# Moving one convolution tap and one query projection in the second layer of a four-layer hybrid model

## The chip, the cores and the metric

The kernel runs on one core of a Trainium2 chip. The metric is the device time of one execution in microseconds (us). The kernel before was timed three times: median 2625.26 us, lowest 2623.77, highest 2625.77. A profile of one more execution, which took 2624.74 us, records each instruction by engine: TensorE (PE, its weight loads PEld), VectorE (DVE), ScalarE (ACT), GpSimdE (POOL) and SyncE's DMA queue (SP). Lines such as L856 are lines of the kernel before.

## The reference

Four layers run over 1040 positions (16 learned ones ahead of 1024 inputs) of width 1024. Each normalises its input, mixes along the sequence, and adds its output. Layers 1 and 4 are sliding window attention, layer 3 is a gated linear recurrence, and layer 2, the one concerned here, is an mLSTM with eight heads. Cut to what matters of it:

```python
def causal_conv(x, w, b):                       # four taps along the sequence
    K = w.shape[0]
    L = x.shape[1]
    xp = jnp.pad(x, ((0, 0), (K - 1, 0), (0, 0)))
    return sum(xp[:, j:j + L] * w[j] for j in range(K)) + b

q, k, v, ig, fg, og, z = _split(u @ w_in, B_SIZES)
qk = jax.nn.silu(causal_conv(jnp.concatenate([q, k], axis=-1), conv_w, conv_b))
...
h = mlstm_chunkwise(qh, kh, vh, log_i, log_f)   # blocks of 128, a state C carried from block to block
h = jax.nn.sigmoid(og) * h
h = rmsnorm(h, h_gain)
return (h * jax.nn.silu(z)) @ w_out
```

## The kernel before, in words

All values are kept transposed, features on the 128 partitions and positions along the free axis. The positions are cut into three chunks of 400, 384 and 256 columns, which hold the blocks 0 to 3, 4 to 6 and 7 to 8 (block 0 has 16 positions, the others 128). A projection (`proj`, L211) makes one tile of 128 features: for each chunk 24 matmuls of 128x128 weights (L228, three products of split operands for each eighth of the input) into one PSUM bank, and then its evacuation function. PSUM has eight banks, handed out by one pool to everything that needs one. Weights are loaded by SP in two halves, then split by ScalarE (the rounded part, `wh`) and VectorE (the remainder, `wl`) at L194 and L195; each of the two has three buffers.

**Order of the work.** TensorE's order is written out by hand: a list of steps, each with a cost, a function and perhaps a weight load to be issued 12 us of cost ahead. `weave` merges two lists in proportion to their costs, `later` puts single steps in at given costs. The instructions of the other engines are put in order when the program is built, by priority (the order in which the code issues them) and by when the build expects their inputs; the steps of a mixer are issued with a priority 40 places ahead. On the chip each engine then works through its order as it stands, and waits where an input is missing.

**A query or key tile** of head h (`conv_proj`, L836) is one projection. The evacuation of a chunk takes a temporary `raw` of three columns more than the chunk. VectorE puts into these three the end of the chunk before (L849, zeros for the first, L847). ScalarE copies the chunk from PSUM into `raw` (L850). VectorE makes the last tap and the bias from it (L853), then adds the three other taps (L856, three times). Then SiLU: ScalarE L400 to L402 (abs, exp, ln), VectorE L403, ScalarE L404 (exp), and the product on VectorE (L860 for queries, L862 with a constant for keys). `raw` and the temporary of the SiLU come from a ring of six. Query tiles have two buffers, key tiles come from a ring of eight rows.

**The mixer of a head** (`mixer`, L875) works on nine blocks. `start` loads two rows, broadcast over the partitions (L881, L882). For each block: s1, the scores k*q (L889) and a transpose of k (L891), and beside it the decay E (VectorE L893, ScalarE L895), W = E times scores (VectorE L897), the scaled queries qw (L900) and keys kw (ScalarE L903). s2, the output product from W (L910) and from the state C (L912), and its normalisation (L914 to L918). s3, the state update: a product (L924) and C on VectorE (L927 for the first block, L929). s4, two transposes (L938) and copies (L940). On TensorE the steps of neighbouring blocks overlap: s1(0), s1(1), s2(0), s3(0), s1(2), s2(1), s3(1), s4(0), and so on.

**The start of the layer.** The head of the layer projects the values of head 0 and the gates (L277). Then come the query and the key tile of head 0, with three steps put in by `later`: the last gate transposes (`gate_turn`), the gate rows (`gate_rows`, L801 to L819: one long row per head on 8 partitions, on ScalarE and VectorE, then written to memory for the broadcasts), and 17 us of cost later the gate columns (`gate_cols`, L829 to L834). Then the mixer of head 0, all but its last three steps, is woven with the query, key and value projections of head 1, and so on for each head.

Of the kernel before, what the change touches and what calls it, by code (L numbers as in the profile page):

```python
# [11 lines left out]
AF = mybir.ActivationFunctionType  # L12
ALU = mybir.AluOpType
# [42 lines left out]
def weave(a, b):  # L56

    ta, tb = sum(x[0] for x in a) + 1e-9, sum(x[0] for x in b) + 1e-9
    out, i, j, ca, cb = [], 0, 0, 0.0, 0.0
    while i < len(a) or j < len(b):  # L60
        if j >= len(b) or (i < len(a) and ca / ta <= cb / tb):
            ca += a[i][0]
            out.append(a[i])
            i += 1
        else:
            cb += b[j][0]
            out.append(b[j])
            j += 1
    return out


def flat(groups):
    return [x for grp in groups for x in grp]
# [13 lines left out]
def later(steps, *events):  # L87

    k, t = 0, 0.0
    for delay, step in events:  # L90
        while k < len(steps) and (t < delay or steps[k][0] == 0.0):
            t += steps[k][0]
            k += 1
        steps.insert(k, step)
        t += step[0]
        k += 1
# [15 lines left out]
def hybrid_kernel(ctx: ExitStack, tc: tile.TileContext, ins, out, layers=(0, 1, 2, 3)):  # L112
    nc = tc.nc
    v, s, g, pe, sp = nc.vector, nc.scalar, nc.gpsimd, nc.tensor, nc.sync
# [11 lines left out]
    def nm(x):  # L126
        ctr[0] += 1
        return f"{x}{ctr[0]}"

    def row():  # L130
        return rpool.tile([P, T], F32, tag="r", name=nm("r"), bufs=ROWS)
# [7 lines left out]
    def tmp():  # L139
        return tpool.tile([P, 404], F32, tag="t", name=nm("t"), bufs=TMPS)  # L140
# [70 lines left out]
    def proj(src, evac, chunks=CHUNKS):  # L211
        st = {}

        def pre():
            st["w"] = weights(src, "m")

        groups = []
        for n, (c0, cn) in enumerate(chunks):
            grp = []
            for part in range(4):  # L220
                def fn(n=n, c0=c0, cn=cn, part=part):
                    if part == 0:
                        st[n] = psj()
                    h, l = st["w"]
                    acc = st[n]
                    for k in (2 * part, 2 * part + 1):
                        for i, (a, b) in enumerate(((h, uh), (h, ul), (l, uh))):
                            pe.matmul(acc[:, :cn], a[:, k, :], b[:, k, c0 : c0 + cn],  # L228
                                      start=(k == 0 and i == 0), stop=(k == KT - 1 and i == 2))
                    if part == 3:  # L230
                        evac(acc, n, c0, cn)

                grp.append([6 * cn * MM, fn, pre if (n == 0 and part == 0) else None])
            groups.append(grp)
        return groups
# [9 lines left out]
    def proj_v(srcs, evac, kind="v"):  # L245

        st = {}
        nc = 256 if kind == "v" else 272
        pieces, k = [], 0
        for src in srcs:  # L250
            n = src.shape[-1] // nc
            pieces.append((k, n, src))
            k += n

        groups = []
        for blocks in CHUNK_BLOCKS:
            grp = []
            for b in blocks:
                c0, cn = blk(b)
                for i, (k0, kn, src) in enumerate(pieces):  # L260
                    def pre(i=i, src=src):
                        st[i] = weights(src, kind)

                    def fn(b=b, c0=c0, cn=cn, i=i, k0=k0, kn=kn):
                        if i == 0:
                            st["a", b] = psj()
                        acc = st["a", b]
                        wh, wl = st[i]
                        for kk in range(kn):
                            k = k0 + kk  # L270
                            if b == 0:
                                for m in (wh, wl):
                                    pe.matmul(acc[:48, :nc], um[0][:, k, :], m[:, kk, :],
                                              start=(k == 0 and m is wh), stop=(k == KT - 1 and m is wl))
                            else:
                                for j, (a, m) in enumerate(((uh, wh), (uh, wl), (ul, wh))):
                                    pe.matmul(acc[:cn, :nc], a[:, k, c0 : c0 + cn], m[:, kk, :],  # L277
                                              start=(k == 0 and j == 0), stop=(k == KT - 1 and j == 2))
                        if i == len(pieces) - 1:
                            evac(acc, b, c0, cn)  # L280

                    grp.append([(2 if b == 0 else 3) * kn * nc * MM, fn, pre if b == 0 else None])
            groups.append(grp)
        return groups
# [113 lines left out]
    def sigmoid_from(z, cn):  # L398
        a = tmp()
        s.activation(a[:, :cn], z, AF.Abs)  # L400
        s.activation(a[:, :cn], a[:, :cn], AF.Exp, scale=-1.0)
        s.activation(a[:, :cn], a[:, :cn], AF.Ln, bias=one)  # L402
        v.scalar_tensor_tensor(a[:, :cn], z, 0.0, a[:, :cn], op0=ALU.min, op1=ALU.subtract)  # L403
        s.activation(a[:, :cn], a[:, :cn], AF.Exp)  # L404
        return a
# [351 lines left out]
    def layer_b(i, j, fin):  # L757
# [78 lines left out]
        def conv_proj(src, mt, mul, key):  # L836
            prev = [None, None]

            def evac(acc, n, c0, cn):
                conv = R["conv"]  # L840
                raw = tmp()
                if n == 0:
                    if mt < 8:
                        R[key] = R["mix"].tile([P, T], F32, tag="q", name=nm("q"), bufs=2)
                    else:
                        R[key] = row()
                    v.memset(raw[:, 0:3], 0.0)  # L847
                else:
                    v.tensor_copy(raw[:, 0:3], prev[0][:, prev[1] : prev[1] + 3])  # L849
                s.copy(raw[:, 3 : 3 + cn], acc[:, :cn])  # L850
                prev[:] = [raw, cn]
                y = R[key][:, c0 : c0 + cn]
                v.tensor_scalar(y, raw[:, 3 : 3 + cn], conv[:, mt, 3:4], conv[:, mt, 4:5],  # L853
                                op0=ALU.mult, op1=ALU.add)
                for q in (2, 1, 0):
                    v.scalar_tensor_tensor(y, raw[:, q : q + cn], conv[:, mt, q : q + 1], y,  # L856
                                           op0=ALU.mult, op1=ALU.add)
                a = sigmoid_from(y, cn)
                if mul == 1.0:
                    v.tensor_tensor(y, y, a[:, :cn], op=ALU.mult)  # L860
                else:
                    v.scalar_tensor_tensor(y, y, mul, a[:, :cn], op0=ALU.mult, op1=ALU.mult)  # L862

            return proj(src, evac)

        def v_evac(h):
            def f(acc, b, c0, cn):
                R["v", h, b] = V = vtile()
                put_v(V, acc, b, cn)
                if h == 0:  # L870
                    gate_evac(acc, b, cn)
                g.memset(V[:cn, 256:257], 1.0)
            return f
# [120 lines left out]
        qg = {h: conv_proj(win[8 * h], h, 1.0, ("q", h)) for h in range(8)}  # L994
        kg = {h: conv_proj(win[8 * h + 1], 8 + h, 128 ** -0.5, ("k", h)) for h in range(8)}
        gsrc = [ins["b_wv0"][j][:, 272 * a : 272 * b] for a, b in ((0, 3), (3, 6), (6, 8))]
        vg = {h: proj_v([win[8 * h + 2], win[8 * h + 3]], v_evac(h)) if h else proj_v(gsrc, v_evac(0), "g") for h in range(8)}
# [14 lines left out]
        for n in (0, 1):  # L1012
            later(head[n + 1], (GATE_LAG, gate_turn(n)))
        head[0].insert(0, [0.0, enter, None])
        body = flat(qg[0]) + flat(kg[0])
        later(body, (GATE_LAG, gate_turn(2)), (0.0, [0.0, gate_rows, None]), (GATE_COLS, [18 * 30, gate_cols, None]))
        for h in range(8):
            mx = mixer(h)
            mx, rest = mx[:-3], mx[-3:]
            if h < 7:  # L1020
                body += weave(mx, flat(qg[h + 1]) + flat(kg[h + 1]) + flat(vg[h + 1]))
                if h < 6:
                    body += weave(rest, gates(h)[:6]) + gates(h)[6:] + flat(zg[h][1]) + flat(outs(oc[h]))
                else:
                    held = rest
            else:
                body += weave(held + mx, gates(6) + flat(zg[6][1]))
# [304 lines left out]
    for pos, i in enumerate(layers):  # L1332
# [10 lines left out]
        if i % 3 == 0:  # L1343
            head, body, oa, ob = layer_a(i, i // 3, tail is None, i == 3, fin)
        elif i % 3 == 1:
            head, body, oa, ob = layer_b(i, i // 3, fin)
        else:
            head, body, oa, ob = layer_c(i, i // 3, fin)
# [155 lines left out]
```

## Time and profile before

| | |
|---|---|
| median of three runs | 2625.26 us |
| the profiled execution | 2624.74 us |
| its span, first to last instruction | 2623.0 us |
| TensorE busy | 2565.2 us, 98% |
| VectorE busy | 1970.6 us, 75% |
| ScalarE busy | 1665.7 us, 64% |
| granted TensorE clock, mean | 0.993 of full |

How to read the profile. A group has line, engine, operation, output and inputs by the program's names, shape and count; then busy time and the mean duration in ns; then the engine's idle time just before, and what ended it. In a timeline a row is start, duration, engine, line and operation, with the idle time before it and its releaser in brackets. A wait row names who waited for whom, the total in us, how often, and the longest. Matmuls are pipelined: a row's duration is longer than the distance to the next one, so steps of TensorE are measured from start to start. Durations of neighbouring VectorE rows overlap by a little under 0.1 us.

### The profile page before, as it was taken

The page shows a single profiled execution, that of the slowest core. Times are in us where ns is not written, and L with a number is a line of the kernel's source. Part 1 is how long each engine was busy: PE and PEld are TensorE (multiplying, and loading weights), DVE is VectorE, ACT ScalarE, POOL GpSimd, SP SyncE. Part 2 cuts the span into 40 slices and gives each one's busy share as a digit, 9 for nine tenths or more (in the row PEclk, how much of TensorE's full clock was granted, in tenths as well). Part 3 has the DMA queues.
Part 4 walks back from the last instruction along what each step waited for, and adds up shares of the span by engine and source line. Part 5 has one row for each costly group of instructions (what it writes and reads, how often), then busy time and mean ns, then how long its engine had stood idle before and what let it go on. Part 6 is the DMA issues. An engine that isn't in the chain of part 4 may idle for free. (4 is left out here: it accounts for less than half of the span.)

```text
span 2623.0 us, 54248 instructions
## 1 busy us (share of the span) xinstructions
PE 2565.2 (98%) x20422; PEld 2484.6 (95%) x20422; DVE 1970.6 (75%) x5296; ACT 1665.7 (64%) x4374; POOL 249.8 (10%) x502
## 2 busy tenths in 40 slices
PE   7999999989999999999999999999999999999999
PEld 5999999989999999999999999999999999999999
DVE  6798798784747474747475688989787978887996
ACT  6776767565454545454545657878585857767772
POOL 2221221000000000000000000100000100321330
PEclk9999999999999999999999999999999999999999
DMA  4212111021111111111111101011110112212112
GB/s 129 68 50 84 55 44 48 22 66 49 42 56 41 57 41 56 42 53 45 53 45 49 49 26 50 26 42 34 34 42 30 38 51 86 59 50 84 55 39 79
DMA packets 82583, 135.92 MB, mean 52 GB/s; under 512 B 12033, under 2 KB 35713, under 8 KB 82321
## 3 DMA queue, kind: packets, MB, share of 16 engines
q1 hardware_dynamic: 82320, 132.45, 16.2%
q8 instruction: 161, 2.64, 0.4%
q14 instruction: 102, 0.83, 0.1%
HBM read 117.56 MB, written 4.26 MB: 46 GB/s over the span
## 5 line engine op out<-in xcount | busy, mean ns | idle before, releaser
L228 PE MATMUL pj<-uh,wh 128*128 128x256 f32 (+2 forms) x2688 | 916.4, 341 | 9.6 <-ACT uh L194 9.6
L228 PE MATMUL pj<-ul,wh 128*128 128x256 f32 (+2 forms) x2688 | 867.9, 323 | 2.2 <-DVE ul L195 1.7
L228 PE MATMUL pj<-uh,wl 128*128 128x256 f32 (+2 forms) x2688 | 864.6, 322 | 0.0
L228 PEld LDWEIGHTS pj<-uh,wh 128*128 128x128 f32 x2688 | 510.2, 190 | 26.8 <-ACT uh L194 13.2
L228 PEld LDWEIGHTS pj<-ul,wh 128*128 128x128 f32 x2688 | 510.5, 190 | 11.1 <-DVE ul L195 5.8
L228 PEld LDWEIGHTS pj<-uh,wl 128*128 128x128 f32 x2688 | 510.0, 190 | 0.0
L194 ACT CAST wh<-wr 128x512 fp32r<-128x512 f32 (+1 forms) x338 | 203.2, 613 | 110.9 <-PE pj L322 32.7
L195 DVE TENSOR_TENSOR wl<-wr,wh 128x512 fp32r<-128x512 f32 (+1 forms) x338 | 233.7, 701 | 51.6 <-ACT wh L194 49.3
L325 DVE TENSOR_TENSOR x<-x,pj 128x384 f32<-128x384 f32 (+2 forms) x480 | 234.7, 508 | 35.0 <-PE pj L322 33.7
L322 PE MATMUL pj<-yh,wh 128*128 128x384 f32 (+2 forms) x768 | 253.0, 329 | 8.0 <-DVE x L325 6.2
L322 PE MATMUL pj<-yh,wl 128*128 128x384 f32 (+2 forms) x768 | 245.2, 319 | 0.0
L322 PE MATMUL pj<-yl,wh 128*128 128x384 f32 (+2 forms) x768 | 245.2, 319 | 0.0
L277 PE MATMUL pj<-wh,uh 128*128 128x256 f32 (+1 forms) x768 | 231.9, 302 | 0.0
L277 PE MATMUL pj<-wl,uh 128*128 128x256 f32 (+1 forms) x768 | 216.5, 282 | 0.0
L277 PE MATMUL pj<-wh,ul 128*128 128x256 f32 (+1 forms) x768 | 216.2, 281 | 0.0
L635 POOL TENSOR_TENSOR Sm<-Sm,s 128x512 f32<-128x512 f32 (+2 forms) x136 | 142.1, 1045 | 449.4 <-DVE s L634 434.5
L632 ACT ACTIVATE Sm<-Sm,s 128x257 f32<-128x257 f32 (+2 forms) x272 | 130.9, 482 | 79.5 <-DVE s L629 75.3
L404 ACT ACTIVATE t<-t 128x384 f32<-128x384 f32 (+2 forms) x240 | 117.9, 491 | 87.8 <-DVE t L403 86.0
L403 DVE SCALAR_TENSOR_TENSOR t<-pj,t 128x384 f32<-128x384 f32 (+2 forms) x192 | 98.7, 514 | 80.0 <-ACT t L402 78.1
L322 PEld LDWEIGHTS pj<-yh,wh 128*128 128x128 f32 x768 | 144.2, 188 | 11.7 <-DVE x L325 7.4
L194 ACT CAST yh<-r 128x384 fp32r<-128x384 f32 (+2 forms) x120 | 57.1, 478 | 151.9 <-PE pj L322 139.8
L277 PEld LDWEIGHTS pj<-wh,uh 128*128 128x128 f32 x768 | 144.6, 188 | 2.1
(255 smaller groups left out, 5423.0 us busy)
## 6 DMA issues: line engine op xcount, KB each, us to landing
wr<-in_b_win SPq DMA_DIRECT2D x124, 256.0 KB, 2.8
wr<-in_a_win SPq DMA_DIRECT2D x80, 256.0 KB, 2.9
wr<-in_c_win SPq DMA_DIRECT2D x64, 256.0 KB, 2.8
wr<-in_a_wout SPq DMA_DIRECT2D x32, 256.0 KB, 2.8
wr<-in_b_wout SPq DMA_DIRECT2D x32, 256.0 KB, 2.8
t<-t SPq DMA_DIRECT2D x104, 48.0 KB, 1.9
cs<-in_rope SPq DMA_DIRECT2D x11, 400.0 KB, 3.4
cs<-in_rope SPq DMA_DIRECT2D x11, 384.0 KB, 3.6
```

Of the source, the lines that this page charges most:

```text
L194: s.copy(h, src)
L195: v.tensor_tensor(l, src, h.bitcast(F32), op=ALU.subtract)
L228: pe.matmul(acc[:, :cn], a[:, k, :], b[:, k, c0 : c0 + cn], start=(k == 0 and i == 0), stop=(k == KT - 1 and i == 2))
L277: pe.matmul(acc[:cn, :nc], a[:, k, c0 : c0 + cn], m[:, kk, :], start=(k == 0 and j == 0), stop=(k == KT - 1 and j == 2))
L322: pe.matmul(acc[:, :cn], a[:, k, mc], b, start=(k == 0 and i == 0), stop=(k == 1 and i == 2))
L325: v.tensor_tensor(x[:, m, c0 : c0 + cn], x[:, m, c0 : c0 + cn], acc[:, :cn], op=ALU.add)
L403: v.scalar_tensor_tensor(a[:, :cn], z, 0.0, a[:, :cn], op0=ALU.min, op1=ALU.subtract)
L404: s.activation(a[:, :cn], a[:, :cn], AF.Exp)
L632: s.activation(Sm[:nq, u, : nk + 1], Sm[:nq, u, : nk + 1], AF.Exp, scale=-1.0, bias=st[:nq, u : u + 1], accum_out=den[:nq, u : u + 1])
L635: g.tensor_tensor(Sm[:nq, :, :nk], Sm[:nq, :, :nk], den[:nq].rearrange("p (u c) -> p u c", c=1).to_broadcast([nq, 2, nk]), op=ALU.mult)
```

## The change

It has two parts, both in the second layer.

The last tap and the bias of the convolution, `raw * w3 + b`, made by VectorE from `raw` at L853, become one ScalarE activation (Identity with a column for scale and one for bias) that reads the PSUM bank itself. The copy into `raw` at L850 stays for the three other taps, which stay on VectorE. This holds for all 16 query and key tiles, three chunks each: 48 instructions.

The projection of head 1's query tile (`qg[1]`) is taken out of the list that is woven with the first mixer, and appended to the query and key tile of head 0, ahead of that mixer. Its weight loads go with it. The mixer of head 0 is then woven with head 1's key and value projections alone. The later heads keep their order.

```diff
@@ conv_proj, evac @@
                 s.copy(raw[:, 3 : 3 + cn], acc[:, :cn])
                 prev[:] = [raw, cn]
                 y = R[key][:, c0 : c0 + cn]
-                v.tensor_scalar(y, raw[:, 3 : 3 + cn], conv[:, mt, 3:4], conv[:, mt, 4:5],
-                                op0=ALU.mult, op1=ALU.add)
+                s.activation(y, acc[:, :cn], AF.Identity, bias=conv[:, mt, 4:5], scale=conv[:, mt, 3:4])
                 for q in (2, 1, 0):
                     v.scalar_tensor_tensor(y, raw[:, q : q + cn], conv[:, mt, q : q + 1], y,
                                            op0=ALU.mult, op1=ALU.add)
@@ layer_b @@
-        body = flat(qg[0]) + flat(kg[0])
+        body = flat(qg[0]) + flat(kg[0]) + flat(qg[1])
         later(body, (GATE_LAG, gate_turn(2)), (0.0, [0.0, gate_rows, None]), (GATE_COLS, [18 * 30, gate_cols, None]))
         for h in range(8):
             mx = mixer(h)
             mx, rest = mx[:-3], mx[-3:]
             if h < 7:
-                body += weave(mx, flat(qg[h + 1]) + flat(kg[h + 1]) + flat(vg[h + 1]))
+                body += weave(mx, (flat(qg[h + 1]) if h else []) + flat(kg[h + 1]) + flat(vg[h + 1]))
```

## The prediction

> **What bounds the kernel now.** I read the busy table first, then the waits of TensorE, then the stretches of time around the change, then three timelines. The busy table:
>
> ```profile
> span 2623.0 us, 54248 instructions
> ...
> PE 2565.2 (98%) x20422; PEld 2484.6 (95%) x20422; DVE 1970.6 (75%) x5296; ACT 1665.7 (64%) x4374; POOL 249.8 (10%) x502
> ```
>
> TensorE is busy for all but 58 us. VectorE and ScalarE have slack on average, so an edit gains only where TensorE waits. The second layer's queries, keys and mixers run from about 520 to 1400 us. The waits of TensorE from 500 to 1400 us hold a single row:
>
> ```profile
> PE pm L889 <- DVE r L862: 8.9, 1, 8.9
> ```
>
> L889 is the first score product of a mixer, L862 the last operation on a chunk of keys. Rows by stretch (length, then busy time of PE, PEld, DVE, ACT, POOL with instruction counts, granted clock, DMA):
>
> ```profile
> 544.00:553.00 9.00, 0.17 (x2) 0.00 (x0) 8.65 (x23) 6.07 (x15) 0.00 (x0) 0.79 0.30 98
> ...
> 544.00:561.55 17.55, 8.67 (x42) 7.39 (x40) 14.41 (x41) 11.77 (x31) 0.00 (x0) 0.81 0.20 65
> ...
> 585.00:600.00 15.00, 15.00 (x121) 14.73 (x119) 8.91 (x29) 8.43 (x23) 0.10 (x1) 1.00 0.19 70
> 700.00:1400.00 700.00, 700.00 (x4662) 684.32 (x4661) 431.17 (x1097) 363.45 (x866) 4.78 (x49) 1.00 0.15 48
> ```
>
> From 700 to 1400 us TensorE is never idle and VectorE is busy 62% of the time, ScalarE 52%. In the 9 us hole VectorE works 8.65 us: it is the late engine there. TensorE's timeline shows the price:
>
> ```profile
> 531.29 0.35 PE L228 MATMUL pj<-uh,wh 128*128 128x400 f32 x1
> ...
> 538.67 0.33 PE L228 MATMUL pj<-uh,wl 128*128 128x384 f32 x1
> ...
> 540.05 0.44 PE L228 MATMUL pj<-uh,wh 128*128 128x384 f32 x1
> ...
> 543.89 0.28 PE L228 MATMUL pj<-uh,wl 128*128 128x256 f32 x1
> 553.05 0.24 PE L889 MATMUL pm<-q,r 128*16 128x16 f32 x2 [8.88 <-DVE r L862]
> ...
> 553.25 0.68 PE L228 MATMUL pj<-uh,wh 128*128 128x400 f32 x1
> ...
> 555.40 0.63 PE L889 MATMUL pm<-q,r 128*128 128x128 f32 x2
> ...
> 555.89 0.45 PE L228 MATMUL pj<-uh,wh 128*128 128x400 f32 x1
> ...
> 571.00 0.38 PE L889 MATMUL pm<-q,r 128*128 128x128 f32 x2
> ...
> 571.24 0.43 PE L228 MATMUL pj<-uh,wh 128*128 128x400 f32 x1
> ...
> 572.41 0.59 PE L910 MATMUL po<-v,W 128*128 128x257 f32 x2
> ```
>
> The first key tile is projected from 531.29 to 544.0 us, with the gate transposes between 538.84 and 540.05 in it: 12.7 - 1.2 = 11.5 us for the projection of one tile. Then nothing for 8.88 us. After the hole the six matmuls from 553.25 to 555.40 take 2.15 us; the same six from 571.24 to 572.41 take 1.17 us. The score step at 555.40 takes 0.49 us to the next projection, the one at 571.00 takes 0.24. So the hole costs 8.88 us, and the slow clock behind it (2.15 - 1.17) + (0.49 - 0.24) = 1.2 us: **10.1 us** in all.
>
> **The move of the second query tile.** It removes no work. The 11.5 us of projection, now woven into the first mixer, stand in the hole: TensorE works from 544.0 to 555.5 us instead of stopping. The score step needs the first chunk of keys, whose last operation is this VectorE row:
>
> ```profile
> 518.42 1.29 DVE L195 TENSOR_TENSOR wl<-wr,wh 128x512 fp32r<-128x512 f32 x2 [7.33 <-ACT wh L194]
> 522.58 0.69 DVE L195 TENSOR_TENSOR wl<-wr,wh 128x512 fp32r<-128x512 f32 x1 [2.86 <-ACT wh L194]
> 523.45 0.69 DVE L195 TENSOR_TENSOR wl<-wr,wh 128x512 fp32r<-128x512 f32 x1 [0.18 <-ACT wh L194]
> ...
> 527.04 0.69 DVE L195 TENSOR_TENSOR wl<-wr,wh 128x512 fp32r<-128x512 f32 x1
> ...
> 529.42 0.67 DVE L195 TENSOR_TENSOR wl<-wr,wh 128x512 fp32r<-128x512 f32 x1
> ...
> 552.43 0.56 DVE L862 SCALAR_TENSOR_TENSOR r<-r,t 128x400 f32<-128x400 f32 x1
> ...
> 553.64 0.16 DVE L897 TENSOR_TENSOR W<-E,pm 16x16 f32<-16x16 f32 x1
> ...
> 561.13 0.42 DVE L862 SCALAR_TENSOR_TENSOR r<-r,t 128x256 f32<-128x256 f32 x1
> ```
>
> The chunk is ready at 552.99 us even without the other edit, 2.5 us ahead of 555.5. So the wait at L889 goes, and so does the 1.2 us of slow clock. The moved tile's weights are the third pair of weight splits (first pair: 518.42, both halves in one row), done at 530.1 us, 14 us before they are used. The loads keep their order among themselves on SP's queue. The next load after the key weights of head 1 needs a buffer that the moved tile frees at 555.5 instead of later, so no load is put back. The two broadcast loads that start the mixer stand 11.5 us later in the written order, and the mixer that wants them starts 2.5 us later (555.5 against 553.05); where SP issues them behind weight loads of head 1 that could go first, they lose that room, and if they came later still, the wait would show as a VectorE wait for a DMA ahead of L897. I cost the loads at nothing: their source, the gate rows, is written long before, and SP has only weight loads beside them. The cover is the 14 us for the weights and the 2.5 us for the broadcasts.
>
> **What is late next.** VectorE does not catch up because TensorE has other work. The keys end at 561.55 us on VectorE, while TensorE left them at 544.0. In its new place the moved tile adds its own evacuation to that queue, ahead of part of the first mixer. The first mixer operation that TensorE needs back is L897 (at 553.64 above), the scores times the decay, wanted by L910. Between the score step and L910 stand two groups of six matmuls and one more score step: 2 x 1.17 + 2 x 0.24 = 2.8 us, so L910 is due at 555.5 + 2.8 = 558.3 us. When VectorE reaches L897 follows from its work, for which these are the prices (sums and means by group, 544 to 561.55 us):
>
> ```profile
> L856 DVE SCALAR_TENSOR_TENSOR r<-t,bcols,r 128x400 f32<-128x400 f32 (+2 forms) x9 | 5.1, 571 | 0.1
> L403 DVE SCALAR_TENSOR_TENSOR t<-r,t 128x400 f32<-128x400 f32 (+2 forms) x3 | 1.5, 514 | 1.4 <-ACT t L402 1.4
> L862 DVE SCALAR_TENSOR_TENSOR r<-r,t 128x400 f32<-128x400 f32 (+2 forms) x3 | 1.5, 513 | 0.0
> L853 DVE TENSOR_SCALAR r<-t,bcols 128x400 f32<-128x400 f32 (+2 forms) x3 | 1.4, 458 | 0.4 <-ACT t L850 0.3
> ...
> L893 DVE SCALAR_TENSOR_TENSOR E<-rb,bcol,caus 128x128 f32<-128x128 f32 (+1 forms) x4 | 1.3, 315 | 0.6 <-ACT kw L903 0.6
> ...
> L853 DVE TENSOR_SCALAR q<-t,bcols 128x400 f32<-128x400 f32 x1 | 0.5, 487 | 0.4 <-ACT t L850 0.4
> ...
> L897 DVE TENSOR_TENSOR W<-E,pm 16x16 f32<-16x16 f32 (+1 forms) x2 | 0.4, 220 | 0.0
> ```
>
> Of the 14.41 us that VectorE is busy from 544 to the end of the keys, four L853 (1.4 + 0.5 = 1.9) go to ScalarE, and about 1.3 us (two L897, two of the four L893, some 0.2 of column work) belongs behind the new place of L897: 11.2 us are left. The first chunk of the moved tile adds three taps and two products, 3 x 0.57 + 2 x 0.51 = 2.7 us. So L897 comes at the earliest at 544.0 + 11.2 + 2.7 = 557.9 us. At the latest it stands behind the three taps of the second chunk too (1.7) and VectorE idles as it did there (17.55 - 14.41 = 3.1): 562.7 us. I take the middle, 560.3, since VectorE did idle in that stretch while the order that the build gives can lie either way. With 0.2 us for L897 itself, L910 starts at 560.5 instead of 558.3: **2.2 us come back**, with 0 and 4.6 as ends. In the hole the clock lost (1 - 0.79) x 9.0 = 1.9 us of full-speed time, which at the half speed of 2.15 against 1.17 is some 4 us: the clock fell about 5 us into the hole, so a wait of 2.2 us should bring no slow matmuls.
>
> [...]
>
> **The first tap on ScalarE.** Here the rows for the price:
>
> ```profile
> L402 ACT ACTIVATE t<-t,one 128x400 f32<-128x400 f32 x40 | 25.1, 628 | 0.6
> L918 ACT ACTIVATE hn<-po,s 128x256 f32<-128x256 f32 x53 | 24.9, 470 | 15.2 <-DVE s L916 15.2
> ...
> L903 ACT ACTIVATE kw<-pm,E 128x128 f32<-128x128 f32 x48 | 17.2, 359 | 17.8 <-DVE W L897 17.8
> ...
> L850 ACT COPY t<-pj 128x400 f32<-128x400 f32 x16 | 7.7, 481 | 6.8 <-PE pj L228 6.8
> ```
>
> It removes 48 L853 from VectorE, 0.46 us each: 22 us. It adds 48 activations from PSUM with a column for scale and one for bias. L918 and L903 read PSUM with one such column: 470 ns at 256 columns, 359 at 128, so 0.87 ns per column and 595 ns at 400; three chunks cost 0.60 + 0.58 + 0.47 = 1.65, sixteen tiles 26 us. Bounds: the copy's 481 ns below, L402's 628 above. Spread over the layer ScalarE goes from 52% to about 55% busy where TensorE is the bound, so neither the 22 nor the 26 us shows in the span. What it does is in the sum above: 1.9 us less in VectorE's queue before L897. Without that, L910 would be 4.1 us late.
>
> [...]
>
> The copy and the activation both read the bank, so it is held longer:
>
> ```profile
> 545.05 0.47 ACT L850 COPY t<-pj 128x400 f32<-128x400 f32 x1
> ...
> 548.75 0.46 ACT L850 COPY t<-pj 128x384 f32<-128x384 f32 x1
> ...
> 554.65 0.34 ACT L850 COPY t<-pj 128x256 f32<-128x256 f32 x1
> ```
>
> The three key chunks leave PSUM up to 11 us after TensorE finished them. At 544.0 they hold three of eight banks, the moved tile takes three more: six, without a wait.
>
> **Sum.** Profiled execution 2624.74 us (span 2623.0 and 1.7 around it); - 8.9 - 1.2 + 2.2 = 2616.8. The median of the runs, 2625.26, is 0.5 above that execution: **2617.3 us**, 0.3% faster. A change of 0.2% (5.3 us) is about what the measurement can tell from none.
>
> **Rivals.** (a) Clean: L897 is reached by 558.1 us because VectorE finds no idle time; nothing comes back: 2615.2. For it: the earliest bound, 557.9. Against it: VectorE waited for ScalarE four times in that stretch (1.4, 0.6, 0.4, 0.4 in the groups). (b) Banks: if no bank is free at 544.0, the moved tile starts when the 545.05 copy (0.47) and the activation behind it (0.60) end, 2.1 us late; its third chunk, 256 of 1040 columns and so 2.8 us before 555.5, was due at 552.7 and waits for the 554.65 copy (0.34) with 0.5 behind it, to 555.5: 2.8 us late in all, 2618.0 with a clean mixer and 2620.2 with the 2.2. For it: the late copies. Against it: two banks to spare. (c) The move does little: most or all of the hole goes over to L910, since the same VectorE queue ends it, 4.6 to 10.1 us, so 2619.7 to 2625.3. It needs L897 between 562.7 and 568, past my latest bound. (d) Slower: the first mixer has one tile fewer woven in (33 us of projection by the written costs instead of 43), its blocks come closer, and the carried state C, which TensorE wants two steps after its product, falls behind a chunk's taps in VectorE's order. Price: three taps and two products, 2.7 us, less some 0.7 to 1 us of room, 1.7 to 2.0 in each of eight blocks: 14 to 16 us, 2629 to 2631; it decides from 10.1 / 8 = 1.3 us per block. Against it: only three key chunks are left to stand in the way, and from 585 us VectorE is busy 8.91 of 15.
>
> **Chances.** Forecast (2615.7 to 2619.7) 0.55; (a) 0.20; (b) 0.10; (c) 0.09; (d) 0.06. Orders on VectorE and ScalarE elsewhere are laid out anew at the build; I allow 2 us either way for that. The range goes from 2613.2, 2 us below (a), to 2622, which takes in (b) and a third of (c); some 0.15 is left out. Faster by over 0.2% (below 2620.0): 0.55 + 0.20 + 0.07 of (b) = 0.82; within: the rest of (b) and (c), 0.12; slower: 0.06.
>
> **What would show it.** Right: no wait at L889; TensorE busy from 544 to 555 us at full clock; a wait of 0 to 4.6 us at the first L910 put down to L897; 48 activations at 0.5 to 0.6 us in place of L853. Wrong: a wait of L228 in the moved tile for ScalarE (b); 8 us or more at L910 (c); waits at L910 or L912 in block after block (d); or a gain that comes from outside 520 to 600 us.

## The result, and the profile after

The changed kernel takes 2615.34 us (median of 5 runs, 2614.55 to 2617.52) against 2625.77 us for the kernel before in the same series (5 runs, 2623.77 to 2630.91): ratio 0.9957, 95% interval 0.9945 to 0.9969. It is faster by 0.43%. The profiled execution took 2615.34 us as well. In the rows of after all lines from L854 on stand one lower than in the kernel before: L855 are the three taps, L859 and L861 the products of queries and keys, L888 the scores, L896 W, L909 the output product from W. L853 is now the tap on ScalarE.

The busy table of after:

```profile
span 2613.6 us, 54261 instructions
...
PE 2565.6 (98%) x20422; PEld 2485.5 (95%) x20422; DVE 1952.1 (75%) x5248; ACT 1689.4 (65%) x4422; POOL 249.1 (10%) x502
```

TensorE does the same work (2565.6 us against 2565.2) in a span 9.4 us shorter. VectorE lost 48 instructions and 18.5 us of busy time, ScalarE gained 48 and 23.7 us (in the busy times an overlap of neighbouring instructions counts once). From 500 to 1400 us TensorE has no wait at all in after. By stretch (the moved tile, then the steady part of the layer; columns as in the prediction):

```profile
542.16:553.66 11.50, 11.50 (x75) 11.37 (x73) 9.63 (x25) 8.89 (x23) 0.00 (x0) 1.00 0.40 132
...
700.00:1400.00 700.00, 700.00 (x4680) 684.48 (x4679) 413.52 (x1052) 376.19 (x888) 4.77 (x49) 1.00 0.15 48
```

From 542.16 to 553.66 us, where the hole was, TensorE works for all of 11.50 us, at the full clock (1.00). Over the steady part VectorE went from 431 to 414 us, ScalarE from 363 to 376, and TensorE is busy throughout as before. Its timeline in after:

```profile
517.60 0.35 PE L228 MATMUL pj<-uh,wh 128*128 128x400 f32 x1
...
542.16 0.35 PE L228 MATMUL pj<-uh,wh 128*128 128x400 f32 x1
...
546.35 0.34 PE L228 MATMUL pj<-uh,wl 128*128 128x400 f32 x1
546.53 0.34 PE L228 MATMUL pj<-uh,wh 128*128 128x384 f32 x1
...
553.66 0.21 PE L888 MATMUL pm<-q,r 128*16 128x16 f32 x2
...
556.53 0.60 PE L909 MATMUL po<-v,W 16*16 16x257 f32 x2
```

The first row is the start of head 0's query tile, the second the start of the moved tile, the third the last matmul of its first chunk, the fourth the start of its second chunk, and then the first mixer follows with no wait in brackets. VectorE over the same time:

```profile
548.96 0.62 DVE L855 SCALAR_TENSOR_TENSOR r<-t,bcols,r 128x384 f32<-128x384 f32 x1 [1.10 <-ACT r L853]
...
551.12 0.57 DVE L861 SCALAR_TENSOR_TENSOR r<-r,t 128x400 f32<-128x400 f32 x1
...
553.94 1.00 DVE L855 SCALAR_TENSOR_TENSOR r<-t,bcols,r 128x256 f32<-128x256 f32 x2 [1.05 <-ACT r L853]
...
555.72 0.15 DVE L896 TENSOR_TENSOR W<-E,pm 16x16 f32<-16x16 f32 x1
...
557.58 0.63 DVE L855 SCALAR_TENSOR_TENSOR q<-t,bcols,q 128x400 f32<-128x400 f32 x1 [0.82 <-ACT q L853]
```

Two things are to be seen. VectorE idles 1.10 and 1.05 us, and there it waits for the new tap on ScalarE. And W (555.72) stands ahead of the first tap of the moved tile (557.58), not behind it. W is done at 555.87, L909 starts at 556.53: 0.66 us of room. ScalarE's order says why:

```profile
547.03 0.54 ACT L400 ACTIVATE t<-r 128x400 f32<-128x400 f32 x1 [1.04 <-DVE r L855]
547.47 0.46 ACT L850 COPY t<-pj 128x384 f32<-128x384 f32 x1
547.83 0.54 ACT L401 ACTIVATE t<-t 128x400 f32<-128x400 f32 x1
548.27 0.66 ACT L853 ACTIVATE r<-pj,bcols 128x384 f32<-128x384 f32 x1
...
555.87 0.40 ACT L400 ACTIVATE t<-r 128x256 f32<-128x256 f32 x1
556.18 0.47 ACT L850 COPY t<-pj 128x400 f32<-128x400 f32 x1
```

In every chunk the copy out of PSUM (L850) comes directly behind L400 of the chunk before it, and L400 needs that chunk's last tap. So the chunks go one behind the other through both engines: taps, L400, copy, L401, new tap, taps. TensorE finished the moved tile's first chunk at about 546.7 us (its last matmul starts at 546.35 and takes 0.34); the copy of that chunk starts at 556.18, 9.5 us later, because the last key chunk stands before it.

To keep what lies outside the layer apart, I measure from the start of head 0's query tile (the matmul at 517.60 above, 519.45 in before) to the last transpose of the last mixer. Its row, of before and of after (ns min/median/max, then first to last start):

```profile
L938 PE MATMUL pt<-ident,hn x144: 207/272/273, 569.6 to 1486.2; 128*128 128x128 f32 x128, 16*128 16x16 f32 x16
```

```profile
L937 PE MATMUL pt<-ident,hn x144: 207/272/274, 566.8 to 1474.5; 128*128 128x128 f32 x128, 16*128 16x16 f32 x16
```

The last starts give 1486.2 - 519.45 = 966.75 us before and 1474.5 - 517.60 = 956.9 after: **9.85 us less, all of it in this layer**. Ahead of the layer the two profiles differ by 1.85 us in after's favour, behind it by 2.3 the other way. Over all kernels below the start varies from 516.7 to 520.7 us: such differences of some us outside the layer have no tie to the edits, and I found no cause for them. Each of these distances comes from one profiled execution.

### The profile page after: what moved, and what is told of

Same layout as the page of the kernel before. It is cut to its first block, busy times and chain, and to the rows that moved or that the text cites. A ratio compares the mean times of both kernels' runs of the same rounds, so it can differ in the third digit from the quotient of the medians.

```text
span 2613.6 us, 54261 instructions
## 1 busy us (share of the span) xinstructions
PE 2565.6 (98%) x20422; PEld 2485.5 (95%) x20422; DVE 1952.1 (75%) x5248; ACT 1689.4 (65%) x4422; POOL 249.1 (10%) x502
## 4 chain that ended last, share of the span: by engine, by line
PE 80%; DVE 9%; ACT 6%; DMA 2%; issue 2%; SPq 1%; POOL 0%; DVEq 0%; ACTq 0%; POOLq 0%
PE pj L228 39%; PE pj L322 16%; PE pj L277 10%; PE po L666 2%; PE pt L647 2%; PE po L909 1%; PE pa L923 1%; PE po L911 1%; PE pm L621 1%; ACT Sm L632 1%; PE pm L622 1%; DVE Sm L629 1%; PE pj L273 1%; PE pm L1161 1%; DMA cs<-in_rope 1%
## 5 line engine op out<-in xcount | busy, mean ns | idle before, releaser
L322 PEld LDWEIGHTS pj<-yh,wh 128*128 128x128 f32 x768 | 144.5, 188 | 11.9 <-DVE x L325 7.3
```

The source lines that it names most:

```text
L322: pe.matmul(acc[:, :cn], a[:, k, mc], b, start=(k == 0 and i == 0), stop=(k == 1 and i == 2))
```

## The experiments

The theory: the move alone fills the hole, which before came of too much work for VectorE ahead of the keys; and nothing comes back at W because the ring of six temporaries, handed out in the order of issue, ties the chunks together, so that the moved tile's evacuation cannot come ahead of W. (The code takes a chunk's `raw` from the ring right behind the SiLU temporary of the chunk before, and L400 is the first to write that one.) The rivals: the tap brings a part of the gain, as the prediction had it; or the ring set the pace in the kernel before as well. "In the layer" is the distance just defined, less after's 956.9 us. The ratios are to runs of the kernel before in the same series, of which there were three. Lines are those of before for e2, e5 and e9b, those of after for the others.

| kernel | in the layer | waits of TensorE, 500 to 1400 us | median | ratio to before, 95% |
|---|---|---|---|---|
| before | +9.85 | 8.9 | 2625.77, 2625.53, 2626.47 (by series) | |
| after | 0 | none | 2615.34 | 0.9957 (0.9945 to 0.9969) |
| e1, tap only | +11.5 | 9.3 | 2626.62 | 1.0007 (0.9998 to 1.0015) |
| e2, move only | +0.3 | 0.3 | 2615.83 | 0.9964 (0.9950 to 0.9977) |
| e3, one chunk moved | +7.2 | 4.9 | 2622.99 | 0.9993 (0.9984 to 1.0002) |
| e9, after with an own ring | +0.4 | none | 2617.65 | 0.9970 (0.9959 to 0.9982) |
| e5, before, two row operations on GpSimdE | +14.6 | 12.4 | 2631.12 | 1.0016 (1.0007 to 1.0025) |
| e9b, before with an own ring | +7.6 | 5.8 | 2625.41 | 0.9997 (0.9988 to 1.0006) |
| e10, two chunks moved | +1.1 | 0.8 and 0.2 | 2617.70 | 0.9968 (0.9956 to 0.9981) |
| e6, query and key tile moved | +1.0 | 0.9 | 2617.55 | 0.9967 (0.9954 to 0.9979) |

### Each part alone

e1 is the kernel before with the tap's edit alone:

```diff
-                v.tensor_scalar(y, raw[:, 3 : 3 + cn], conv[:, mt, 3:4], conv[:, mt, 4:5],
-                                op0=ALU.mult, op1=ALU.add)
+                s.activation(y, acc[:, :cn], AF.Identity, bias=conv[:, mt, 4:5], scale=conv[:, mt, 3:4])
```

> The kernel before with the tap on ScalarE alone, the second query tile left in the first mixer. Theory (the chunk-by-chunk chain sets VectorE's pace: a chunk leaves PSUM only after the chunk before has its three taps, and the tap on ScalarE lengthens that chain by as much as it takes off VectorE): the wait of TensorE at the first score step stays, 8.5 to 9.5 us, and the time is that of before within 1 us, ratio 0.9995 to 1.0005. Rival (VectorE's load sets it, as the prediction had it): four L853 less ahead of the first key chunk, the wait falls by 1.5 to 1.9 us to about 7, ratio about 0.9993.

A row of VectorE's timeline in e1, and the hole in TensorE's:

```profile
548.15 0.62 DVE L855 SCALAR_TENSOR_TENSOR r<-t,bcols,r 128x384 f32<-128x384 f32 x1 [1.10 <-ACT r L853]
```

```profile
550.93 0.24 PE L888 MATMUL pm<-q,r 128*16 128x16 f32 x2 [9.28 <-DVE r L861]
```

The hole stays and is 0.4 us longer (9.28 against 8.88). VectorE does less, and now idles for the tap: counted from the start of the query tile, the first key chunk is ready after 34.0 us, against 33.5 before, and of these VectorE works 25.4 us, against 28.1.

e2 is the kernel before with the two lines of the move alone:

```diff
-        body = flat(qg[0]) + flat(kg[0])
+        body = flat(qg[0]) + flat(kg[0]) + flat(qg[1])
...
-                body += weave(mx, flat(qg[h + 1]) + flat(kg[h + 1]) + flat(vg[h + 1]))
+                body += weave(mx, (flat(qg[h + 1]) if h else []) + flat(kg[h + 1]) + flat(vg[h + 1]))
```

> The kernel before with the moved query tile alone, the tap left on VectorE. Theory (the move brings all of it): no wait at the first score step and none or under 0.5 us at the first product with W; time within 1 us of the changed kernel, ratio to before 0.996. Rival (the prediction's sum without the tap): the first product with W is late by about 4 us, so a ratio of about 0.9977; a weaker form, four L853 against the 0.66 us of room that the changed kernel has there, 1.2 us.

VectorE and TensorE in e2 (lines as in before):

```profile
558.50 0.15 DVE L897 TENSOR_TENSOR W<-E,pm 16x16 f32<-16x16 f32 x1
558.71 0.49 DVE L853 TENSOR_SCALAR q<-t,bcols 128x400 f32<-128x400 f32 x1
```

```profile
556.39 0.21 PE L889 MATMUL pm<-q,r 128*16 128x16 f32 x2
...
559.26 0.60 PE L910 MATMUL po<-v,W 16*16 16x257 f32 x2
```

No hole and no wait at L910; the one wait of TensorE, 0.3 us, is at L912 for the state C. W again stands ahead of the moved tile's first tap. With the tile starting at 520.33, W comes 38.2 us after it, in after 555.72 - 517.60 = 38.1. So the move carries the whole gain, and the tap neither helps nor hurts in what these runs can tell: the intervals of e2 and after overlap, and that of e1 takes in 1.

### How much of the tile is needed

e3 and e10 are the changed kernel with only the first one or two chunks of the tile moved, the rest left in the first mixer:

```diff
-        body = flat(qg[0]) + flat(kg[0]) + flat(qg[1])
+        body = flat(qg[0]) + flat(kg[0]) + flat(qg[1][:1])
...
-                body += weave(mx, (flat(qg[h + 1]) if h else []) + flat(kg[h + 1]) + flat(vg[h + 1]))
+                body += weave(mx, flat(qg[h + 1] if h else qg[1][1:]) + flat(kg[h + 1]) + flat(vg[h + 1]))
```

(e10: `[:2]` and `[2:]`.)

> The changed kernel with only the first chunk (400 columns, 4.4 us) of the second query tile ahead of the first mixer, its other two chunks woven into it. Theory (TensorE simply waits for the first key chunk, which is ready about 9.2 us after the key tile is projected): a wait of 9.2 - 4.4 = 4.8 us at the first score step; and if the clock falls only some 5 us into a hole, matmuls at full pace behind it, so the gain is half of the change's or a little more: ratio to before 0.998. [...]

> The changed kernel with the first two chunks (8.6 us) of the second query tile ahead of the first mixer and the third woven into it. Theory (TensorE needs about 9.2 us of cover, and a short wait brings no slow clock): a wait of 0.5 to 0.8 us at the first score step, nothing slow behind it, time 0 to 1.5 us above the changed kernel, ratio to before 0.996 to 0.9965. Rival (the first W has no more than the room of 0.66 us, which a denser start of the mixer uses up): a second wait at the first product with W, 1 us or more, ratio 0.997.

The waits of TensorE in e3, and in e10:

```profile
PE pm L888 <- DVE r L861: 4.9, 1, 4.9
```

```profile
PE pm L888 <- DVE r L861: 0.8, 1, 0.8
PE po L911 <- DVE C L926: 0.2, 1, 0.2
```

One chunk (4.4 us of matmuls) takes 4.4 us off the hole of 9.3 that e1 has, two leave 0.8, three none. The hole is filled microsecond for microsecond. e3's stretches, the hole and the 8 us behind it:

```profile
545.78:550.71 4.93, 0.01 (x1) 0.00 (x0) 3.83 (x12) 4.17 (x10) 0.00 (x0) 0.89 0.03 10
550.71:558.71 8.00, 8.00 (x32) 6.73 (x33) 4.64 (x15) 4.78 (x14) 0.00 (x0) 0.64 0.20 68
```

The clock behind the hole is down to 0.64: e3 loses 7.2 us in the layer, 2.3 more than its wait. In e10 the 8 us behind the wait of 0.8 run at 1.00.

### The ring

e9 is the changed kernel, e9b the kernel before, each with `raw` of three tiles (head 0's query and key, head 1's query) taken from another ring, of three buffers, that nothing else uses in this stretch:

```diff
-                raw = tmp()
+                raw = (tpool.tile([P, 404], F32, tag="yh", name=nm("cr"), bufs=YS) if mt in (0, 8, 1) else tmp())
```

> The changed kernel with the copies of the three tiles around the hole (query and key of head 0, query of head 1) in a ring of their own of three buffers, so that a chunk's copy need not wait for the chunk before; VectorE's order then has the first chunk of the moved tile ahead of the first W. Theory (in the changed kernel VectorE idles for ScalarE, so with the idle time gone it can take the moved chunk too): the first key chunk is ready 1 to 3 us earlier, W within 1 us of where it was, no wait of TensorE from 500 to 1400 us, time that of the changed kernel within 1 us. Rival (the changed kernel lost nothing only because W stood ahead of the moved chunk): W 2 to 4 us later, a wait of 1.5 to 3.5 us at the first product with W.

ScalarE, VectorE and TensorE in e9:

```profile
549.28 0.47 ACT L850 COPY cr<-pj 128x400 f32<-128x400 f32 x1
...
552.48 0.40 ACT L400 ACTIVATE t<-r 128x256 f32<-128x256 f32 x1
```

```profile
548.05 0.57 DVE L861 SCALAR_TENSOR_TENSOR r<-r,t 128x400 f32<-128x400 f32 x1
...
551.26 0.63 DVE L855 SCALAR_TENSOR_TENSOR q<-cr,bcols,q 128x400 f32<-128x400 f32 x1
...
557.18 0.15 DVE L896 TENSOR_TENSOR W<-E,pm 16x16 f32<-16x16 f32 x1
```

```profile
557.98 0.60 PE L909 MATMUL po<-v,W 16*16 16x257 f32 x2
```

The order changes as the theory of the ring has it: the copy of the moved tile's first chunk (549.28) is now ahead of L400 of the last key chunk (552.48), and the taps of the moved chunk (from 551.26 on) are ahead of W. The first key chunk is ready 29.6 us after the start of the query tile (548.62 - 519.04), 4.5 earlier than in after; of these 4.5 us, 2.7 are less idle time of VectorE, and 1.8 less work ahead of that chunk, mostly two weight splits fewer. Yet W comes at 557.18 - 519.04 = 38.1 us, as in after. From the start of the moved tile to W VectorE works 13.1 us of 13.6 in e9 and 11.4 of 13.6 in after: what the idle time gave, the work of the moved chunk took. So the place of the moved chunk behind W is not what keeps L909 from waiting. The layer takes the same time.

> The kernel before with the copies of the same three tiles in a ring of their own, tap on VectorE, nothing moved. Theory (there VectorE is busy almost throughout, it idles only 0.9 us between 538 and 553 us, so a looser chain has little to give): the wait at the first score step 7.5 to 9 us, ratio 0.9993 to 1. Rival (the shared ring is what makes the hole): the first key chunk 4 us earlier as in the changed kernel with its own ring, the wait 5 us or less, ratio 0.998.

The hole in e9b is 5.8 us, 3.1 us shorter than in before, where I had expected it to stay. From the start of the query tile to the first key chunk VectorE works 28.1 us and idles 5.4 in before; in e9b it works 26.2 and idles 4.3. So 1.1 of the 3.1 us is idle time, and 2.0 are three weight splits that the new order puts behind that chunk: in the kernel before, too, it was the order that goes with the shared ring, and not an amount of work that had to be done first, that made a third of the hole. That VectorE is busy 8.53 of the 8.88 us of the hole did not show this: 5.1 of its 5.4 us of idle time lay ahead of the hole, and busy time does not say whether the work had to stand there. In the layer e9b gains 2.2 us; in its time that cannot be told from nothing.

### VectorE's work or the chain

e5 is the kernel before with two operations on the gate rows given to GpSimdE, which was to take 2 x 1.22 us off VectorE ahead of the keys:

```diff
-            v.tensor_tensor(bs[:8, :], li[:8, :], a[:8, :], op=ALU.subtract)
-            v.tensor_tensor(a[:8, :], a[:8, :], m[:8, :], op=ALU.subtract)
+            g.tensor_tensor(bs[:8, :], li[:8, :], a[:8, :], op=ALU.subtract)
+            g.tensor_tensor(a[:8, :], a[:8, :], m[:8, :], op=ALU.subtract)
```

> The kernel before with two of the long gate-row subtractions (L810, L811, 1.2 us each on VectorE) on GpSimdE. Theory (in the kernel before the hole is VectorE's load up to the first key chunk, the gate rows in it): VectorE has 2.3 us less, the wait at the first score step falls by 1.5 to 2.3 us, to about 7, unless GpSimdE's rows come so late that ScalarE, which has their exponential at the head of its queue, falls behind by as much; ratio about 0.9993. Rival (VectorE's load does not matter, the chain of chunks alone does): the wait stays at 8.5 to 9.5 us or grows.

GpSimdE and ScalarE in e5:

```profile
534.48 2.70 POOL L810 TENSOR_TENSOR r<-r,r 8x1040 f32<-8x1040 f32 x1 [25.23 <-DVE r L808]
537.25 4.01 POOL L811 TENSOR_TENSOR r<-r,r 8x1040 f32<-8x1040 f32 x1
```

```profile
541.30 0.21 ACT L815 ACTIVATE r<-r 8x16 f32<-8x16 f32 x1 [5.93 <-POOL r L811]
```

The same two operations in before, and two others of VectorE in e5:

```profile
535.33 1.22 DVE L810 TENSOR_TENSOR r<-r,r 8x1040 f32<-8x1040 f32 x1
...
536.97 1.22 DVE L811 TENSOR_TENSOR r<-r,r 8x1040 f32<-8x1040 f32 x1
```

```profile
534.73 2.66 DVE L853 TENSOR_SCALAR q<-t,bcols 128x384 f32<-128x384 f32 x1
...
538.93 2.88 DVE L195 TENSOR_TENSOR wl<-wr,wh 128x512 fp32r<-128x512 f32 x1
```

The expectation missed: the hole grew to 12.4 us. GpSimdE takes 2.70 and 4.01 us for what VectorE does in 1.22 each, and ScalarE, whose next instruction in order wants the second result, stands still for 5.93 us with the copies of the chunks behind it: L815 starts 22.5 us after the start of the query tile, against 18.8 in before, and the hole is 3.5 us longer. VectorE was not relieved either. Its L853 of 2.66 us and its weight split of 2.88 us run beside the two operations on GpSimdE and end 0.2 and 0.6 us after them; in before no L853 takes more than 0.49 us, and from 500 to 1400 us no such weight split more than 0.69 (in other layers up to 1.52, at 335.02 us, beside a GpSimdE operation of 1.27). So VectorE was spared 2.4 us and lost 4.4. That GpSimdE held it up is what the times suggest; no run tests it. Work taken off VectorE thus gained nothing, and the experiment does not say what 2.4 us less of VectorE's work would bring with both engines undisturbed; that stays open.

### More of the same

e6 is the changed kernel with head 1's key tile moved as well, so that the first mixer has only the values woven in:

```diff
-        body = flat(qg[0]) + flat(kg[0]) + flat(qg[1])
+        body = flat(qg[0]) + flat(kg[0]) + flat(qg[1]) + flat(kg[1])
...
-                body += weave(mx, (flat(qg[h + 1]) if h else []) + flat(kg[h + 1]) + flat(vg[h + 1]))
+                body += weave(mx, (flat(qg[h + 1]) + flat(kg[h + 1]) if h else []) + flat(vg[h + 1]))
```

> The changed kernel with head 1's key tile ahead of the first mixer as well, which is then woven with head 1's values alone (22 us of projection by the written costs instead of 33). Theory (the state and W come back in time as long as VectorE is not behind, and each chunk of the key tile gives it more time than work): no wait at the first score step, at most 1 us of waits in the mixer; time within 1.5 us of the changed kernel. Rival (d) of the prediction (a mixer with less woven in is late block after block): waits at products with W or C in several blocks, 3 us or more in all.

The waits in e6:

```profile
PE po L909 <- ACT t L404: 0.9, 1, 0.9
```

One wait of 0.9 us, and +1.0 us in the layer. Even with two tiles fewer in it the first mixer does not fall behind block after block. None of the variants is clearly faster than the changed kernel: the intervals of e2, e6, e9 and e10 all overlap its own.

## Why the prediction was right

**The hole and the slow clock behind it.** Right: 10.1 us were to go, 9.85 went in the layer, at full clock, with no wait at L888, and e2 shows that the move does it. The times of TensorE came out to within 0.1 us: the first scores 36.06 us after the start of the query tile (36.05 predicted, 555.5 - 519.45), L909 38.93 us (38.85 predicted, 558.3 - 519.45).

**What is late next.** This step failed. It put W at 560.3, 40.85 us after the start of the query tile, and let 2.2 us come back at L910. Measured: 38.1 us, and nothing comes back; that is 2.7 us earlier than the middle I took and 0.3 earlier than the lower end (557.9, or 38.45). The sum took the moved chunk's 2.7 us as certain and part of 3.1 us of idle time on top, and in the runs the one stands where the other does not. Up to the start of the moved tile it had 24.55 us, which is what after and e9 show (24.56 and 24.57), and its 11.2 us of VectorE's work before W was about right. In after VectorE works 11.4 us from there to W, none of it for the moved chunk's taps, and idles 2.2: 24.56 + 11.4 + 2.2 = 38.1. In e9 it works 13.1 us, three taps and one product of the moved chunk among them, and idles 0.5: 24.57 + 13.1 + 0.5 = 38.1. One edit, the ring, changed both. Taking the middle between an end without idle time and one with all of it assumed the moved chunk and the idle time together; rival (a), "clean", with 2615.2 us, is what happened (2615.34), though not for its reason: it wanted VectorE without idle time. The median is 2.0 us below the forecast, about the 2.2 that did not come back; but that much also varies outside the layer, so that the total of (a) came out to 0.1 us is partly luck.

**The first tap.** That "neither the 22 nor the 26 us shows in the span" held. The price of the tap was too low. The groups of the new tap on query chunks in after (sum and mean ns):

```profile
L853 ACT ACTIVATE q<-pj,bcols 128x400 f32<-128x400 f32 x8 | 5.5, 684 | 0.0
L853 ACT ACTIVATE q<-pj,bcols 128x384 f32<-128x384 f32 x8 | 5.4, 678 | 0.0
...
L853 ACT ACTIVATE q<-pj,bcols 128x256 f32<-128x256 f32 x8 | 4.4, 555 | 0.0
```

684 ns at 400 columns, not 595, and above my upper bound of 628; over all 48 it comes to 30.5 us (5.5 + 5.4 + 4.4 and, for the keys, 5.4 + 5.3 + 4.5) instead of 26. (ScalarE's busy time rose by 23.7 us, since it counts overlaps once.)

The claim that it takes 1.9 us out of VectorE's queue ahead of W, so that without it L910 would be 4.1 us late, was wrong. Without it (e2) there is no wait at L910 either, and W comes at 38.2 us against 38.1. From the start of the moved tile to W VectorE works 12.2 us and idles 1.4 in e2; in after it works 11.4 and idles 2.2. ScalarE's L401 and the tap came into the chain between the copy and the other taps, and VectorE idles for them in place of the work that it lost.

**Weights, loads and banks at nothing.** Right for TensorE: no wait of it for weights, for the broadcasts or for a bank shows in the layer, though the moved tile's first chunk stood in its bank 9.5 us before its copy. ScalarE does wait for weight loads there (21.7 us in all, 23.3 in before) and VectorE for a broadcast (11.7 us, 11.9 in before), which costs TensorE nothing.

**The clock.** That "the clock fell about 5 us into the hole, so a wait of 2.2 us should bring no slow matmuls" was not put to the test at 2.2, but its ground is wrong as a rule: the hole of 4.9 us in e3 was followed by a stretch at 0.64.

**The rivals.** Banks (b): no such wait. The hole goes over to L910 (c): no; the due time was met with 0.66 us to spare. Denser mixer, slower (d): no; after has no wait in any block, and e6, with two tiles taken from the mixer, a single one of 0.9 us.

## What to carry to other kernels

A hole at the start of a stage, behind a chain of evacuations, is best filled with TensorE work that is ready and depends on nothing in that chain; size it by the hole (here 8.9 us of hole, 11.5 us of tile), and look first at what comes due behind it. Before you take work off a busy engine, see whether it is its work or its waiting that makes it late, over the whole chain and not only in the hole, and whether all of that work has to stand there: here a shared ring of temporaries and two engines in strict order made a chain in which an operation moved to the other engine only changed who idles (VectorE 2.2 us ahead of W instead of 1.4). And when two delays may exclude each other, do not take the middle of a range whose upper end has both.

## What was not expected of the hardware

The time at the slow clock did not follow the length of the hole. The stretches of the holes, and of the 8 us behind each, in before, e1, e5 and e9b:

```profile
544.17:553.05 8.88, 0.00 (x1) 0.00 (x1) 8.53 (x23) 6.07 (x15) 0.00 (x0) 0.78 0.30 96
553.05:561.05 8.00, 8.00 (x38) 7.09 (x38) 5.21 (x17) 5.70 (x16) 0.00 (x0) 0.82 0.10 33
```

```profile
541.65:550.93 9.28, 0.00 (x1) 0.01 (x1) 8.18 (x22) 7.17 (x19) 0.00 (x0) 0.75 0.35 111
550.93:558.93 8.00, 8.00 (x31) 6.80 (x32) 4.73 (x16) 5.31 (x15) 0.00 (x0) 0.65 0.19 66
```

```profile
543.47:555.90 12.43, 0.01 (x1) 0.00 (x0) 10.99 (x29) 8.95 (x25) 0.00 (x0) 0.68 0.46 144
555.90:563.90 8.00, 8.00 (x32) 6.84 (x33) 4.68 (x16) 4.91 (x15) 0.00 (x0) 0.65 0.00 0
```

```profile
545.40:551.19 5.79, 0.00 (x1) 0.00 (x1) 5.79 (x17) 4.70 (x14) 0.00 (x0) 0.71 0.37 138
551.19:559.19 8.00, 8.00 (x37) 7.25 (x38) 6.57 (x21) 5.71 (x15) 0.00 (x0) 0.79 0.31 98
```

In before the granted clock is 1.00 up to 549.0 us, 4.8 us into the hole, 0.63 in the half microsecond from there, 0.50 from 549.5 to 555.5, 0.54 in the next half microsecond, and 1.00 again from 556.0 on. With 0.50 taken for the slow clock in the other runs too, which is an estimate, the time spent in it is (1 - clock) x length / 0.5, in the hole and behind it together: 6.8 us in before, 10.2 in e1, 6.8 in e3, 13.6 in e5, 6.7 in e9b. Three of the five are about equal, at holes of 8.88, 4.93 and 5.79 us; what sets these times the runs do not show. A longer hole thus did not cost more behind it in proportion: before's 8.88 us left 2.9 us at the slow clock, e3's 4.93 us left 5.8, since there the clock fell only 1.1 us before the hole ended. By the same estimate it fell between 2.4 us (e9b) and 5.0 us (before) into the hole. What e1 loses in the layer beyond before (1.65 us) is of the size that this gives: 0.4 us of longer hole, and 5.6 instead of 2.9 us at half the clock behind it, which is 1.4.
